# First attention of a two-layer encoder: rope sums bound behind maxima, sum and stacking in separate steps, and the low part of moved pairs on VectorE alone

## The chip, the cores and the metric

The kernel runs on one core of a Trainium2 chip. The metric is the device time of one execution in microseconds, as the median of several runs. The engines are called PE (matmul; PEld is its weight load), DVE (VectorE), ACT (ScalarE), POOL (GpSimd) and SP (SyncE, which here only issues DMAs).

## The reference

An encoder of two layers for one sequence of 1024 tokens with 1024 features in float32. Layer 0 is a differential attention with 8 heads, layer 1 a latent attention (MLA). The change touches layer 0 alone:

```python
proj = h @ w_in                                   # 1024 x 4096
q, k, v, z = split(proj)
q = _rope(q.reshape(b, s, 16, 64), positions)     # 8 heads, two halves of 64 each
k = _rope(k.reshape(b, s, 16, 64), positions)

def block(qb):
    sc = einsum('bqhcd,bkhcd->bhcqk', qb, k) * scale      # c = 0, 1
    p = softmax(sc, axis=-1)
    p = p[:, :, 0] - lam * p[:, :, 1]
    return einsum('bhqk,bkhd->bqhd', p, v)

o = _rmsnorm(o, subln_g) * (1.0 - lambda_init)
o = o.reshape(b, s, 1024) * silu(z)
return o @ w_out

# _rope: concatenate([x1 * cos - x2 * sin, x2 * cos + x1 * sin])
```

## The kernel before

Float32 products run on PE as three matmuls of split operands (`mm3`, L203 to L205): high x high, low x high, high x low. So every operand has a high part, a copy rounded on ACT, and a low part, the difference, on DVE or POOL. For the weights these are `wh` (ACT, L253) and `wl` (POOL, L254). A strip of weights is projected into a PSUM bank `acc`; the strips of the next head's k, q and z are woven as `fill` between the attention tiles of the head before.

A head of layer 0 has eight query tiles of 128 rows, in four pairs `qp`. `q_tile` does for c = 0 and 1 the scores `s` (L905, a PSUM bank of 128x1024 for each c, two in all), the negated maximum `nm` (DVE, L433) and the exponential (ACT, L436; for c = 0 into the tile `e`, for c = 1 in place). The combine (DVE, L911 to L913) then makes p0 - lam x p1 from both, and so is the last reader of the second score bank.

The combined tile must be transposed for the product with v (`pv`). Most pairs go over PE: transposes `tr` (L414), high part `pth` (ACT, L416), low part `ptl` (DVE, L419). The first pair of each half of a head is mostly "moved" (class `Mate`): `move` transposes 32x32 blocks on DVE into `eT` (L1079) and writes them to DRAM, `fetch` reads them back as `pr`, `high` copies the two high halves on ACT (L1097) and, one tile later, `low` subtracts the two low halves, kh = 0 on DVE (L1116) and kh = 1 on POOL (L1113). The pv follows one tile after that. There are 13 moved pairs in layer 0. Layer 1 uses the same class.

A strip of q or k that is done goes through the rope: `rope` copies it to `rp_raw` (ACT, L345 or L347), swaps its quarters by four DMAs into `rp_sw` (L349) and multiplies it by the cosines (POOL, L350). `rot` multiplies the swapped one by the sines (POOL, L355). `fin` adds both on DVE (L359, here "the rope sum"). Then `stack_k` or `stack_q` puts high and low parts into the operand of the scores (`ks`; `qa`, `qb`): copies on ACT (L367, L368, L375, L376), differences on POOL (L369, L370, L377, L378). These steps are spaced by `side`, a queue of which one entry is taken at each tick of the projection stream: three empty ticks, `rot`, three empty ticks, then sum and stacking together.

The engines' orders are set by a list scheduler over the program, with a few bindings. `mk` holds marked instructions, and `behind("V")` lets the next instruction be issued only after the one marked V: at any time the last maximum, low part of a transposed tail, combine, or 32x32 transpose. `in_turn` keeps POOL's instructions in the order of the program.

Of the kernel before, what the change touches and what calls it, by code (L numbers as in the profile page):

```python
# [37 lines left out]
DEF = 7  # L38
ROT = 3
# [54 lines left out]
def f32v(ap):  # L94
    return ap.bitcast(F32)
# [3 lines left out]
def trunk(ctx: ExitStack, tc: tile.TileContext, A, out):  # L99
    nc = tc.nc  # L100
    SP, PE, V, S, G = nc.sync, nc.tensor, nc.vector, nc.scalar, nc.gpsimd
# [29 lines left out]
    def bank(tag, name, shape=None):  # L131
        nonlocal turn
        if tag == "acc":
            turn += 1
            if (turn - 1) % (2 + NB.get("accx", 0)) < 2:
                return psa.tile([P, HF], F32, name=name, tag="acc", bufs=2)
            tag = "accx"
        return ps.tile(shape or [P, HF], F32, name=name, tag=tag, bufs=NB[tag])
# [60 lines left out]
    def pin(ins):  # L199
        return tc.keep_in_program_order(ins) if pinned[0] else ins  # L200
# [9 lines left out]
    mk = {}  # L210

    def behind(eng):

        return tc.issue_after(mk[eng]) if eng in mk else nullcontext()

    def in_turn(ins):

        return tc.keep_in_program_order(ins) if mk else ins
# [105 lines left out]
    side = Side()  # L324
# [13 lines left out]
    def rope(rp, acc, half, scale, eng=G):  # L338

        cs = slice(half * HF, half * HF + HF)  # L340
        raw = rp.tile([P, HF], F32, name="rp_raw", tag="rp", bufs=6)
        sw = rp.tile([P, HF], F32, name="rp_sw", tag="rp", bufs=6)
        r = rp.tile([P, HF], F32, name="rp_r", tag="rp", bufs=6)
        if scale == 1.0:
            S.copy(raw, acc)  # L345
        else:
            S.mul(raw, acc, scale)  # L347
        for q in range(4):
            SP.dma_start(sw[q * 32 : q * 32 + 32], raw[(q ^ 1) * 32 : (q ^ 1) * 32 + 32])  # L349
        r_ = eng.tensor_mul(r, raw, cosT[:, cs])  # L350
        if eng is G:
            in_turn(r_)

        def rot():
            in_turn(G.tensor_mul(sw, sw, sinT[:, cs]))  # L355

        def fin():
            with behind("V"):
                V.tensor_add(r, r, sw)  # L359
            return r  # L360

        return rot, fin

    def stack_k(t, r):

        with behind("S"):
            S.copy(t[0:64, 0, :], r[0:64])  # L367
            S.copy(t[64:128, 1, :], r[64:128])  # L368
        in_turn(G.tensor_sub(t[64:128, 0, :], r[0:64], f32v(t[0:64, 0, :])))  # L369
        in_turn(G.tensor_sub(t[0:64, 1, :], r[64:128], f32v(t[64:128, 1, :])))  # L370

    def stack_q(qa, qb, r, slot=None):

        with behind("S"):
            S.copy(qa[0:64, 0, :], r[0:64])  # L375
            S.copy(qa[64:128, 1, :], r[64:128])  # L376
        in_turn(G.tensor_sub(qb[0:64, 0, :], r[0:64], f32v(qa[0:64, 0, :])))  # L377
        in_turn(G.tensor_sub(qb[64:128, 1, :], r[64:128], f32v(qa[64:128, 1, :])))  # L378

        def swap():  # L380
            for t in (qa, qb):
                for to, at, c in ((slice(64, 128), slice(0, 64), 0), (slice(0, 64), slice(64, 128), 1)):
                    with behind("SP") if slot is not None else nullcontext():
                        SP.dma_start(f32v(t[to, c, :]), f32v(t[at, c, :]))

        if slot is None:
            swap()
        else:
            prep.setdefault(slot, []).append(swap)
# [40 lines left out]
    def softmax_part(ap_, s_ps, zs, bufs, tag="e"):  # L430

        nm = sm.tile([P, 1], F32, name="nm")
        mk["V"] = V.reduce_max(nm, s_ps, axis=AX.X, negate=True).ins  # L433
        e = ap_.tile([P, T], F32, name="e", tag=tag, bufs=bufs) if ap_ else s_ps
        with tc.issue_after(mk.pop("H")) if "H" in mk else nullcontext():
            ex = S.activation(e, s_ps, AF.Exp, bias=nm, scale=1.0, accum_out=zs)  # L436
            pin_last(ex)
            mk["S"] = ex.ins
        return e
# [369 lines left out]

    KS, QS, GZ = {}, {}, {}  # L810

    def k_done(h):
        def f(acc, half):
            rot, fin = rope(wp, acc, half, 1.0, G if h else V)

            def g():
                t = a0a.tile([P, 2, HF], F32R, name="ks", tag="ks", bufs=4)
                stack_k(t, fin())
                KS.setdefault(h, [None, None])[half] = t

            side.add(*[None] * ROT, rot, *[None] * (DEF - 1 - ROT), g)
        return f

    def q_done(h):
        def f(acc, half):
            rot, fin = rope(wp, acc, half, SC0, G if h else V)

            def g():
                qa = a0a.tile([P, 2, HF], F32R, name="qa", tag="qs", bufs=4)
                qb = a0a.tile([P, 2, HF], F32R, name="qb", tag="qs", bufs=4)  # L830
                stack_q(qa, qb, fin(), now[0] + 1 if h and half else None)
                QS.setdefault(h, [None, None])[half] = qa, qb

            side.add(*[None] * ROT, rot, *[None] * (DEF - 1 - ROT), g)
        return f

    def silu_gate(tp, acc):
# [19 lines left out]
    for h in range(NH):  # L857
        items += [(strip0(1, h), h0, k_done(h)), (strip0(0, h), h0, q_done(h)), (strip0(2, h), h0, z_done(h))]
    with tc.issue_after(h_last):
        k_done(0)(kacc, 0)  # L860
# [34 lines left out]
    def q_tile(h, half, ti, zz, ep, mid=lambda i: None, tag="e"):  # L895

        ql = slice(ti * P, (ti + 1) * P)
        zs = [zz[:, ti : ti + 1], sm.tile([P, 1], F32, name="z1")]
        es = []
        qa, qb = QS[h][half]  # L900
        for c in range(2):
            s_ps = bank("sc", "s", [P, T])
            for src, fst in ((qa, True), (qb, False)):
                for kc in range(2):
                    pin(PE.matmul(s_ps[:, kc * HF : (kc + 1) * HF], src[:, c, ql], KS[h][kc][:, c, :], start=fst, stop=not fst))  # L905
            with tc.issue_after(combined[-1]) if c == 0 and combined else nullcontext():
                es.append(softmax_part(None if c else ep, s_ps, zs[c], 1 if ep is a0a or tag != "e" else 2, tag))
            mid(c)
        e0, e1 = es
        z0, z1 = zs  # L910
        V.reciprocal(z1, z1)  # L911
        V.tensor_scalar(z1, z1, z0, neglam[:, 0:1], op0=ALU.mult, op1=ALU.mult)
        combined.append(V.scalar_tensor_tensor(out=e0, in0=e1, scalar=z1[:, 0:1], in1=e0, op0=ALU.mult, op1=ALU.add).ins)  # L913
        if mk:
            mk["V"] = combined[-1]
        return e0

    first, combined = [], []
    for tt in range(8):
        if tt == V_LATE:  # L920
            psum("ps2", sc=2, tr=1, pv=1)
            zz0 = sm.tile([P, 4], F32, name="zz")
            first += [zz0, q_tile(0, 0, 0, zz0, a0a)]
        for _ in range(MODS[tt]):
            next(mods_g)
        for t in pend[2 * tt : 2 + 2 * tt] if tt > 1 else ():
            with tc.issue_after(store_v.last):
                t()
        v0_tile(tt, 1, wv1)
        if tt == HOLD:  # L930
            with tc.issue_after(store_v.last):
                for raw, src in held:
                    SP.dma_start(raw, src)
# [135 lines left out]
    class Mate(Tail):  # L1069
# [6 lines left out]

        def move(self, t, e):
            eT = self.c["pool"].tile([P, D], F32, name="eT", tag="eT", bufs=self.c["nT"])
            mk["V"] = V.transpose(eT.rearrange("p (c k j) -> p c k j", c=4, j=32), e.rearrange("p (k c i) -> p c k i", c=4, i=32)).ins  # L1079
            mk["SP"] = SP.dma_start(self.store[t], eT).ins  # L1080

        def fetch(self):
# [23 lines left out]
        def low(self, eng=V):  # L1106
            if eng is V and self.done:
                return
            self.done = True
            for kh in range(2):  # L1110
                r, (hi, lo) = self.views(kh)
                if kh == 0 if eng is G else kh == 1 and self.c["l"] == 0:
                    in_turn(G.tensor_sub(lo, r, f32v(hi)))  # L1113
                else:
                    with behind("V"):
                        V.tensor_sub(lo, r, f32v(hi))  # L1116

    tails, hooks = [None, None], []
    now, prep, post, due = [0], {}, {}, {}
# [58 lines left out]
    def attn0(h, fills, extra=None, late=None):  # L1178
# [11 lines left out]
        for qp in range(4):  # L1190
# [5 lines left out]
            for t in range(2):  # L1196
# [15 lines left out]
                if early:  # L1212
                    e0 = first.pop()
                else:
                    own = qp % 2 == t == 0
                    e0 = q_tile(h, half, (qp * 2 + t) % 4, zz, a0a if own else a0b, mid, "e" if own or moved or qp % 2 else "eT")
# [968 lines left out]
```

## Time and profile before

| | |
|---|---|
| runs | 1449.73, 1452.91, 1455.47 us (median 1452.91) |
| profiled execution | 1454.32 us, its span 1452.5 us |
| mean granted clock of PE | 0.980 |
| PE busy in the span | 1369.5 us (94%) |
| DVE, ACT, POOL busy | 956.3 (66%), 739.0 (51%), 647.2 (45%) us |
| first attention with its projections | about 144 to 720 us of the span |

A row of the profile names the line, the engine, the operation and the tiles (out<-in, buffer numbers left out). In a timeline row the first two numbers are the start and the duration in us, and a bracket holds the idle time of the engine ahead of the instruction and what ended it. PEclk is the clock granted to PE as a share of full speed.

### The profile page before, as it was taken

The numbers are of one execution on the slowest core, as the hardware profiler recorded it, in microseconds if no ns is written. First come the engines' busy times: TensorE is split into PE (matmuls) and PEld (weight loads), VectorE is DVE, ScalarE is ACT, GpSimd is POOL, SyncE is SP. The second block draws the span as 40 slices with busy tenths as digits, with TensorE's granted clock in tenths as the row PEclk, the third lists the DMA queues.
The fourth block names the chain that finished last, engine by engine and source line by source line (L and its number), as shares of the span: only waits on it lengthen the run. The fifth ranks groups of instructions, "written<-read, shape, count | busy, mean of one in ns | idle before, by whom it ended". The sixth has DMA issues, their size and how long they took to land.

```text
span 1452.5 us, 20216 instructions
## 1 busy us (share of the span) xinstructions
PE 1369.5 (94%) x7046; PEld 1142.3 (79%) x7046; DVE 956.3 (66%) x1352; ACT 739.0 (51%) x1264; POOL 647.2 (45%) x497
## 2 busy tenths in 40 slices
PE   9999889999798899899899999999999999999997
PEld 7778678777687778778778778887888888887886
DVE  7657867776576676777735597515777777664355
ACT  6622356655465555566534555334555555554442
POOL 4325156655474656565364125523133241413562
PEclk9999899999999999899999999999999999999999
DMA  9877845464445355433774313248777887777563
GB/s 350 257 229 239 256 111 143 133 185 119 115 144 157 115 160 145 136 97 102 261 257 142 131 59 108 93 139 240 191 212 205 234 243 202 187 225 232 197 218 143
DMA packets 165624, 258.24 MB, mean 178 GB/s; under 512 B 20369, under 2 KB 85009, under 8 KB 165522
## 3 DMA queue, kind: packets, MB, share of 16 engines
q1 hardware_dynamic: 165522, 256.94, 59.2%
q8 instruction: 56, 0.92, 0.3%
q14 instruction: 46, 0.38, 0.1%
HBM read 159.42 MB, written 73.86 MB: 161 GB/s over the span
## 4 chain that ended last, share of the span: by engine, by line
PE 62%; DVE 11%; DMA 9%; ACT 5%; POOL 5%; issue 5%; SPq 2%; DVEq 0%; POOLq 0%; ACTq 0%
PE s L1872 8%; PE acc L205 6%; PE acc L203 6%; PE acc L204 6%; PE s L905 5%; PE oacc L203 4%; PE oacc L205 4%; PE oacc L204 4%; PE tr L414 3%; PE pv L204 3%; PE pv L205 3%; PE pv L203 3%; DVE nm L433 2%; DVE ada L476 2%; PE zacc L203 1%
## 5 line engine op out<-in xcount | busy, mean ns | idle before, releaser
L433 DVE TENSOR_REDUCE nm<-s 128x1 f32<-128x1024 f32 x192 | 232.8, 1214 | 64.6 <-PE s L905 40.1
L436 ACT ACTIVATE e<-s,nm 128x1024 f32<-128x1024 f32 x128 | 143.1, 1118 | 173.5 <-DVE nm L433 173.1
L254 POOL TENSOR_TENSOR wl<-wraw,wh 128x512 fp32r<-128x512 f32 (+2 forms) x82 | 104.2, 1274 | 127.0 <-ACT wh L253 111.9
L416 ACT CAST pth<-tr 128x512 fp32r<-128x512 f32 x148 | 87.0, 588 | 143.9 <-PE tr L414 143.0
L205 PE MATMUL acc<-h0h,wl 128*128 128x512 f32 x360 | 145.3, 404 | 15.6 <-POOL wl L254 15.6
L204 PE MATMUL pv<-ptl,vt 128*128 128x256 f32 x512 | 147.5, 288 | 8.8 <-POOL ptl L1113 8.7
L203 PE MATMUL acc<-h0h,wh 128*128 128x512 f32 x360 | 149.7, 416 | 2.7 <-DVE v_hl L393 1.7
L203 PE MATMUL pv<-pth,vt 128*128 128x256 f32 x512 | 147.9, 289 | 0.1
L205 PE MATMUL pv<-pth,vt 128*128 128x256 f32 x512 | 146.5, 286 | 0.0
L204 PE MATMUL acc<-h0l,wh 128*128 128x512 f32 x360 | 143.8, 400 | 0.0
L419 DVE TENSOR_TENSOR ptl<-tr,pth 128x512 fp32r<-128x512 f32 x148 | 101.4, 685 | 62.1 <-ACT pth L416 61.4
L1275 POOL TENSOR_TENSOR wol<-wor,woh 128x512 fp32r<-128x512 f32 x64 | 85.6, 1360 | 79.6 <-ACT woh L1274 72.5
L204 PEld LDWEIGHTS pv<-ptl,vt 128*128 128x128 f32 x512 | 99.1, 194 | 14.7 <-POOL ptl L1113 10.0
L414 PE MATMUL tr<-ident,e 128*128 128x128 f32 x592 | 91.1, 277 | 18.8 <-DVE ptl L419 18.5
L414 PEld LDWEIGHTS tr<-ident,e 128*128 128x128 f32 x592 | 71.9, 142 | 44.3 <-DVE ptl L419 18.2
L203 PEld LDWEIGHTS pv<-pth,vt 128*128 128x128 f32 x512 | 98.8, 193 | 5.0 <-ACT pth L416 0.5
L205 PEld LDWEIGHTS pv<-pth,vt 128*128 128x128 f32 x512 | 99.5, 194 | 0.0
L205 PEld LDWEIGHTS acc<-h0h,wl 128*128 128x128 f32 x360 | 69.3, 192 | 34.2 <-POOL wl L254 18.7
L905 PE MATMUL s<-ks,qa 128*128 128x512 f32 x256 | 85.3, 415 | 10.1 <-ACT e L436 4.9
L436 ACT ACTIVATE s<-s,nm 128x1024 f32<-128x1024 f32 x64 | 69.9, 1092 | 30.0 <-DVE nm L433 29.9
L913 DVE SCALAR_TENSOR_TENSOR e<-s,z,e 128x1024 f32<-128x1024 f32 x64 | 82.1, 1284 | 1.8
L905 PE MATMUL s<-ks,qb 128*128 128x512 f32 x256 | 81.8, 401 | 1.6 <-POOL o L965 1.6
(635 smaller groups left out, 3557.1 us busy)
## 6 DMA issues: line engine op xcount, KB each, us to landing
pS<-eT SPq DMA_DIRECT2D x54, 512.0 KB, 3.0
pr<-pS SPq DMA_DIRECT2D x108, 256.0 KB, 5.9
ada<-in_ada_ss SPq DMA_DIRECT2D x32, 512.0 KB, 7.2
wraw<-in_w_s SPq DMA_DIRECT2D x64, 256.0 KB, 3.0
vS<-v_hl SPq DMA_DIRECT2D x32, 512.0 KB, 4.8
vt<-vS SPq DMA_DIRECT2D x32, 512.0 KB, 5.4
wor<-in_w_out SPq DMA_DIRECT2D x64, 256.0 KB, 3.3
rp_sw<-rp_raw SPq DMA_DIRECT2D x168, 64.0 KB, 2.4
```

What stands on the lines that cost most here:

```text
L203: pin(PE.matmul(psum, ah, bh, start=first, stop=False))
L204: pin(PE.matmul(psum, ah, bl, start=False, stop=False))
L205: mm = PE.matmul(psum, al, bh, start=False, stop=last)
L254: sub = (lo_on or (V if pair_of else G)).tensor_sub(l_[:, :n], raw[:, :n], f32v(h_[:, :n]))
L414: pin(PE.transpose(tr[:, j, :], p[:, kt * P : (kt + 1) * P], ident))
L416: cp = S.copy(pth[kh][:, :, dst], tr)
L419: mk["V"] = V.tensor_sub(ptl[kh][:, :, dst], tr, f32v(pth[kh][:, :, dst])).ins
L433: mk["V"] = V.reduce_max(nm, s_ps, axis=AX.X, negate=True).ins
L436: ex = S.activation(e, s_ps, AF.Exp, bias=nm, scale=1.0, accum_out=zs)
L905: pin(PE.matmul(s_ps[:, kc * HF : (kc + 1) * HF], src[:, c, ql], KS[h][kc][:, c, :], start=fst, stop=not fst))
L1275: in_turn(G.tensor_sub(lo, raw, f32v(hi)))
L1872: pin(PE.matmul(s_ps[:, kc * HF : (kc + 1) * HF], lhs, rhs(kc), start=i == 0, stop=i == 4))
```

## The change

Three things change in layer 0.

1. For the heads 1 to 7, `in_two` takes the rope sum out of the entry that stacks: one empty tick after `rot`, the sum; another, the stacking. So the sum is written two ticks earlier in the program, and the stacking where it was. For head 0 nothing changes.
2. The combine and, in layer 0, the 32x32 transpose are marked "C" and no longer "V". The rope sums, bound behind "V", are thus bound behind maxima and tails' low parts only.
3. `Mate.low` in layer 0 does both halves on DVE, bound behind "C". Layer 1 stays as it was.

The core of the diff:

```diff
--- before.py
+++ after.py
@@ -809,29 +809,46 @@
 
     KS, QS, GZ = {}, {}, {}
 
+    def in_two(h, first_, second):
+
+        def both():
+            first_()
+            second()
+
+        if h:
+            side.add(None, first_, None, second)
+        else:
+            side.add(*[None] * (DEF - 1 - ROT), both)
+
     def k_done(h):
         def f(acc, half):
             rot, fin = rope(wp, acc, half, 1.0, G if h else V)
 
+            r = []
+
             def g():
                 t = a0a.tile([P, 2, HF], F32R, name="ks", tag="ks", bufs=4)
-                stack_k(t, fin())
+                stack_k(t, r[0])
                 KS.setdefault(h, [None, None])[half] = t
 
-            side.add(*[None] * ROT, rot, *[None] * (DEF - 1 - ROT), g)
+            side.add(*[None] * ROT, rot)
+            in_two(h, lambda: r.append(fin()), g)
         return f
 
     def q_done(h):
         def f(acc, half):
             rot, fin = rope(wp, acc, half, SC0, G if h else V)
 
+            r = []
+
             def g():
                 qa = a0a.tile([P, 2, HF], F32R, name="qa", tag="qs", bufs=4)
                 qb = a0a.tile([P, 2, HF], F32R, name="qb", tag="qs", bufs=4)
-                stack_q(qa, qb, fin(), now[0] + 1 if h and half else None)
+                stack_q(qa, qb, r[0], now[0] + 1 if h and half else None)
                 QS.setdefault(h, [None, None])[half] = qa, qb
 
-            side.add(*[None] * ROT, rot, *[None] * (DEF - 1 - ROT), g)
+            side.add(*[None] * ROT, rot)
+            in_two(h, lambda: r.append(fin()), g)
         return f
 
     def silu_gate(tp, acc):
@@ -912,7 +929,7 @@
         V.tensor_scalar(z1, z1, z0, neglam[:, 0:1], op0=ALU.mult, op1=ALU.mult)
         combined.append(V.scalar_tensor_tensor(out=e0, in0=e1, scalar=z1[:, 0:1], in1=e0, op0=ALU.mult, op1=ALU.add).ins)
         if mk:
-            mk["V"] = combined[-1]
+            mk["C"] = combined[-1]
         return e0
 
     first, combined = [], []
@@ -1076,7 +1093,7 @@
 
         def move(self, t, e):
             eT = self.c["pool"].tile([P, D], F32, name="eT", tag="eT", bufs=self.c["nT"])
-            mk["V"] = V.transpose(eT.rearrange("p (c k j) -> p c k j", c=4, j=32), e.rearrange("p (k c i) -> p c k i", c=4, i=32)).ins
+            mk["V" if self.c["l"] else "C"] = V.transpose(eT.rearrange("p (c k j) -> p c k j", c=4, j=32), e.rearrange("p (k c i) -> p c k i", c=4, i=32)).ins
             mk["SP"] = SP.dma_start(self.store[t], eT).ins
 
         def fetch(self):
@@ -1109,10 +1126,10 @@
             self.done = True
             for kh in range(2):
                 r, (hi, lo) = self.views(kh)
-                if kh == 0 if eng is G else kh == 1 and self.c["l"] == 0:
+                if eng is G and kh == 0:
                     in_turn(G.tensor_sub(lo, r, f32v(hi)))
                 else:
-                    with behind("V"):
+                    with behind("V" if self.c["l"] else "C"):
                         V.tensor_sub(lo, r, f32v(hi))
 
     tails, hooks = [None, None], []
```

Line numbers behind the first place of the diff are larger by 17 now (the combine L913 is L930, the low part L1116 is L1133, the transpose L1079 is L1096). POOL's list loses 13 rows, the `ptl<-pr,pth` of the moved pairs; what is left keeps its order but for a few neighbours. PE's order stays as it was but for two swaps of neighbours.

DVE at the seventh tile of head 0, before: the low half of a moved pair, the transpose of the next moved tile, the two maxima of a tile with a rope sum between them, then the combine.

```order
L1116 TENSOR_TENSOR ptl<-pr,pth 128x1024
L1079 STREAM_TRANSPOSE eT<-e 128x1024
L433 TENSOR_REDUCE nm<-s 128x1
L359 TENSOR_TENSOR rp_r<-rp_r,rp_sw 128x512
L433 TENSOR_REDUCE nm<-s 128x1
L911 RECIPROCAL z_1847<-z_1847 128x1
L912 TENSOR_SCALAR z_1847<-z_1847,zz,neglam 128x1
L913 SCALAR_TENSOR_TENSOR e<-s,z_1847,e 128x1024
```

DVE at the same place now:

```order
L1133 TENSOR_TENSOR ptl<-pr,pth 128x1024 x2
L1096 STREAM_TRANSPOSE eT<-e 128x1024
L359 TENSOR_TENSOR rp_r<-rp_r,rp_sw 128x512
L433 TENSOR_REDUCE nm<-s 128x1 x2
L928 RECIPROCAL z_1848<-z_1848 128x1
L929 TENSOR_SCALAR z_1848<-z_1848,zz,neglam 128x1
L930 SCALAR_TENSOR_TENSOR e<-s,z_1848,e 128x1024
L433 TENSOR_REDUCE nm<-s 128x1
```

The second low half has come in, and the rope sum stands ahead of both maxima.

DVE in head 2, from the second maximum of the tile that follows a moved pair, before (L911 to L913 are the combine):

```order
L911 RECIPROCAL z_3237<-z_3237 128x1
L912 TENSOR_SCALAR z_3237<-z_3237,zz,neglam 128x1
L913 SCALAR_TENSOR_TENSOR e<-s,z_3237,e 128x1024
L359 TENSOR_TENSOR rp_r<-rp_r,rp_sw 128x512
L433 TENSOR_REDUCE nm<-s 128x1
L1025 TENSOR_TENSOR sl_f<-zz 128x4
```

DVE at the same place now:

```order
L433 TENSOR_REDUCE nm<-s 128x1 x2
L359 TENSOR_TENSOR rp_r<-rp_r,rp_sw 128x512
L928 RECIPROCAL z_3237<-z_3237 128x1
L929 TENSOR_SCALAR z_3237<-z_3237,zz,neglam 128x1
L930 SCALAR_TENSOR_TENSOR e<-s,z_3237,e 128x1024
L433 TENSOR_REDUCE nm<-s 128x1 x2
```

The rope sum, which stood behind the combine, stands ahead of it, directly behind the maxima.

ACT in head 5, from the exponentials of a tile to the high part of a weight strip, before (`zth` is the tanh of the gate, `qa` the stacking of q):

```order
L436 ACTIVATE e,zz<-s,nm 128x1024
L436 ACTIVATE s,z_4895<-s,nm 128x1024
L375 CAST qa<-rp_r 64x512
L376 CAST qa<-rp_r 64x512
L841 ACTIVATE zth<-acc 128x512
L253 CAST wh<-wraw 128x512
```

ACT at the same place now:

```order
L436 ACTIVATE e,zz<-s,nm 128x1024
L416 CAST pth<-tr 128x4x128
L436 ACTIVATE s,z_4895<-s,nm 128x1024
L858 ACTIVATE zth<-acc 128x512
L375 CAST qa<-rp_r 64x512
L376 CAST qa<-rp_r 64x512
L253 CAST wh<-wraw 128x512
```

The tanh has gone ahead of the two `qa` copies, and a tail's copy between the exponentials.

## The prediction

> **What bounds the kernel now.** First the page (busy time by engine), then the waits of PE, the stretches and the groups of instructions, all for the first attention (144 to 720 us), where the whole change lies; at last the order of time around each wait of PE there.
>
> ```profile
> PE 1369.5 (94%) x7046; PEld 1142.3 (79%) x7046; DVE 956.3 (66%) x1352; ACT 739.0 (51%) x1264; POOL 647.2 (45%) x497
> ```
>
> PE is busy for 94%. So no engine's total can decide here, only the gaps and the slow clock of PE. The waits, "engine line <- released by: us in total, times, longest":
>
> ```profile
> PE acc L205 <- POOL wl L254: 15.6, 6, 6.9
> PE tr L414 <- DVE ptl L419: 10.8, 8, 3.0
> PE pv L204 <- POOL ptl L1113: 8.7, 3, 3.3
> PE s L905 <- ACT e L436: 4.9, 4, 1.8
> PE ssq L1022 <- ACT rp_raw L347: 4.1, 2, 3.0
> ```
>
> The instruction that the change takes off POOL (L1113) releases PE three times, 8.7 us. POOL's weight splits cost more, 15.6 us. The stretches (busy us and instructions of each engine, granted clock, DMA):
>
> ```profile
> 206.04:209.45 3.41, 3.41 (x13) 3.02 (x13) 2.82 (x2) 1.01 (x2) 2.13 (x3) 0.50 0.34 109
> 345.99:352.81 6.82, 6.21 (x20) 5.44 (x21) 2.51 (x2) 2.17 (x4) 6.82 (x6) 0.50 0.29 77
> 209.50:345.90 136.40, 127.02 (x683) 107.20 (x681) 105.66 (x139) 82.43 (x140) 78.52 (x62) 1.00 0.55 148
> 144.00:720.00 576.00, 520.49 (x2717) 435.79 (x2715) 412.51 (x549) 321.72 (x545) 317.28 (x245) 0.96 0.53 149
> ```
>
> PE idles 576.00 - 520.49 = 55.5 us here. Between those two stalls the clock is 1.00; behind them it is 0.50 for 3.41 and 6.82 us. At half the clock, half of PE's busy time is lost: 3.41/2 + 6.21/2 = 4.8 us. DVE is busy 412.5 of 576, so 13 more subtractions fit in its total; where they stand decides. The groups (out<-in xcount | busy, mean ns | idle before, releaser):
>
> ```profile
> L1113 POOL TENSOR_TENSOR ptl<-pr,pth 128x1024 fp32r<-128x1024 f32 x13 | 31.7, 2442 | 12.9 <-ACT pth L1097 12.8
> L359 DVE TENSOR_TENSOR rp_r<-rp_r,rp_sw 128x512 f32<-128x512 f32 x28 | 26.7, 954 | 24.6 <-POOL rp_sw L355 24.6
> L1116 DVE TENSOR_TENSOR ptl<-pr,pth 128x1024 fp32r<-128x1024 f32 x13 | 22.5, 1734 | 0.0
> ```
>
> **The change, part by part.** POOL loses 13 x 2.442 = 31.7 us; DVE gains 13 x 1.2 to 1.73 = 16 to 22 us (bounds: the quickest row of L1116, below, and its mean). And DVE's rope sums, which wait 24.6 us for POOL's products in all, move in its order, two ticks earlier and past combines or maxima: whoever stood behind no sum now stands behind a waiting one. No instruction or DMA is added; PE's order hardly changes. I went through the places where PE waits, with the new order on the old durations.
>
> A, head 0, tile 6:
>
> ```profile
> 200.40 1.18 DVE L433 TENSOR_REDUCE nm<-s 128x1 f32<-128x1024 f32 x1
> 206.63 1.75 DVE L359 TENSOR_TENSOR rp_r<-rp_r,rp_sw 128x512 f32<-128x512 f32 x1 [5.04 <-POOL rp_sw L355]
> 203.02 2.33 POOL L1113 TENSOR_TENSOR ptl<-pr,pth 128x1024 fp32r<-128x1024 f32 x1
> 205.31 1.28 POOL L355 TENSOR_TENSOR rp_sw<-rp_sw,sinT 128x512 f32<-128x512 f32 x1
> 205.41 0.39 PE L204 MATMUL pv<-ptl,vt 128*128 128x256 f32 x1 [3.34 <-POOL ptl L1113]
> 208.71 0.97 PE L905 MATMUL s<-ks,qa 128*128 128x512 f32 x2
> ```
>
> The stall of 3.34 goes. But the sum now stands ahead of the maximum of 200.40. Without L1113 the product ends at 203.02 + 1.28 = 204.3, the sum 0.7 to 1.75 later (205 to 206), the maximum at 206.2 to 207.2, the exponential that frees the score bank 1.1 after that. So the scores of 208.71 start at about 208.3, whatever PE saved ahead of them. They gain 0.4; the new stall, of about 4 us, costs clock behind it, as the old one did (up to 1.7, I take 0.8): **+0.4** (bounds -1.5 to +2).
>
> B, head 1:
>
> ```profile
> 275.21 0.39 PE L204 MATMUL pv<-ptl,vt 128*128 128x256 f32 x1 [2.32 <-POOL ptl L1113]
> 277.68 2.01 DVE L359 TENSOR_TENSOR rp_r<-rp_r,rp_sw 128x512 f32<-128x512 f32 x1 [2.27 <-POOL rp_sw L355]
> ```
>
> The stall of 2.32 goes; the sum comes ahead of the combine, which stood ahead of it. With L1113's 2.33 off POOL's queue the sum ends at 276 to 277.4, the combine at 278 to 279.2, and frees the second score bank then. Of 2.32 remain **-1.0** (bounds -2.3 and 0).
>
> C, head 2:
>
> ```profile
> 344.40 1.28 DVE L913 SCALAR_TENSOR_TENSOR e<-s,z,e 128x1024 f32<-128x1024 f32 x1
> 350.29 2.04 DVE L359 TENSOR_TENSOR rp_r<-rp_r,rp_sw 128x512 f32<-128x512 f32 x1 [4.61 <-POOL rp_sw L355]
> 344.20 2.34 POOL L1113 TENSOR_TENSOR ptl<-pr,pth 128x1024 fp32r<-128x1024 f32 x1
> 346.60 0.58 PE L204 MATMUL pv<-ptl,vt 128*128 128x256 f32 x1 [3.04 <-POOL ptl L1113]
> 354.52 0.63 PE L905 MATMUL s<-ks,qa 128*128 128x512 f32 x2
> ```
>
> Stall and slow clock go: 3.04 + 6.21/2 = 6.1 us, so PE would be at the scores of 354.52 by 348.4. Their bank is freed by the combine, now behind the sum: 350.3 - 2.3 = 348.0 for its start, done at 348.7 to 350.0, combine at 350.5 to 351.8. PE waits 2.1 to 3.4: **-3.2** (bounds -6.1 and -2.7).
>
> D, POOL's weight splits, heads 3 to 5:
>
> ```profile
> 376.27 1.22 DVE L1116 TENSOR_TENSOR ptl<-pr,pth 128x1024 fp32r<-128x1024 f32 x1
> 376.45 2.17 POOL L378 TENSOR_TENSOR qb<-rp_r,qa 64x512 fp32r<-64x512 f32 x1
> 380.02 0.79 PE L205 MATMUL acc<-h0h,wl 128*128 128x512 f32 x1 [6.90 <-POOL wl L254]
> 454.81 0.50 PE L205 MATMUL acc<-h0h,wl 128*128 128x512 f32 x1 [4.79 <-POOL wl L254]
> 533.05 0.50 PE L205 MATMUL acc<-h0h,wl 128*128 128x512 f32 x1 [1.77 <-POOL wl L254]
> 450.53 0.60 ACT L841 ACTIVATE zth<-acc 128x512 f32<-128x512 f32 x1
> ```
>
> In these three the split comes ahead of L1113 in POOL's queue already, so nothing is gained. But the qb subtraction beside L1116 takes 2.17 where the same form takes 1.28 (the L355 row, twice the partitions): DVE's subtraction of two SBUF operands and POOL's hold each other up. A second one just behind the first does it again, about 1.05 each time, 3.2 in all (bounds 0 and 3 x 1.22). In heads 4 and 5 ACT's order also sets the gate's tanh (0.60) ahead of the exponential or of the qa casts; that, and what it waits for itself, I put at 0.9 each (0.6 to 1.5). **+5.0** (bounds 0 and +6.7).
>
> The Trainium skill bears on this ("SBUF — State Buffer", section "SBUF: two separate sides"): the port pair that VectorE and GpSimd share is an exclusive lock, held for a whole instruction, when a VectorE instruction with two SBUF inputs meets a GpSimd one that reads SBUF. The trace agrees in kind (2.17 for 1.28). By the rule each second subtraction would cost its full 1.22, and the sum would be 0.5 us higher.
>
> E, heads 4 and 5, where L1113 delayed no one:
>
> ```profile
> 502.42 1.28 DVE L913 SCALAR_TENSOR_TENSOR e<-s,z,e 128x1024 f32<-128x1024 f32 x1
> 505.62 1.76 DVE L359 TENSOR_TENSOR rp_r<-rp_r,rp_sw 128x512 f32<-128x512 f32 x1 [1.92 <-POOL rp_sw L355]
> 505.63 0.62 PE L905 MATMUL s<-ks,qa 128*128 128x512 f32 x2
> 575.10 1.23 DVE L433 TENSOR_REDUCE nm<-s 128x1 f32<-128x1024 f32 x1 [0.69 <-PE s L905]
> 581.27 1.74 DVE L359 TENSOR_TENSOR rp_r<-rp_r,rp_sw 128x512 f32<-128x512 f32 x1 [4.94 <-POOL rp_sw L355]
> 578.05 1.11 ACT L436 ACTIVATE e<-s,nm 128x1024 f32<-128x1024 f32 x1
> ```
>
> In head 4 the combine of 502.42 falls behind the sum of 505.62: done at 508.1 or later, so the scores of 505.63 start 2.5 later; a wait of 1.06 behind them takes some of it: **+1.5** (bounds 0 and 2.5). In head 5 the maximum of 575.10 falls behind the sum of 581.27, and its exponential of 578.05 with it. Both ran while DVE and ACT were free; now 1.23 + 1.11 = **+2.3** lies on the way to the next scores (bounds 0 and 3.8).
>
> F, earlier maxima and tails, no longer behind a combine or a transpose:
>
> ```profile
> 184.62 0.63 PE L414 MATMUL tr<-ident,e 128*128 128x128 f32 x4 [1.31 <-DVE ptl L419]
> 234.85 0.73 PE L905 MATMUL s<-ks,qa 128*128 128x512 f32 x2 [1.33 <-ACT e L436]
> ```
>
> Of 184.62 I credit 0.9 and of 234.85 all 1.3. Of the wait group tr <- ptl (10.8 over 8), what is left without 1.31 and the longest is 6.5 over six, 1.1 each; the new order serves two of these, 1.7. **-3.9** (bounds -5 and 0).
>
> Sum: 0.4 - 1.0 - 3.2 + 5.0 + 1.5 + 2.3 - 3.9 = **+1.1 us**. The profiled execution took 1454.32 us (its span 1452.5), the median of the runs is 1452.91, 1.4 below; so 1455.4 there, and 1454.0 on the median's scale.
>
> **The rivals.** R1, nobody misses DVE: the waits on L1113 (8.7), the clock behind two of them (4.8) and F (3.9) all come back, and the port costs nothing: 1452.9 - 17.4 = 1435.5. For it: DVE has 160 us free here, and a sum that no longer waits for L1113 is ready 2.3 us sooner. Against it: in A, B and C the sum still waits, by up to 3 us, with a maximum or combine behind it. It decides if POOL's products are done before the combine or maximum is. By the Trainium skill ("TensorE: Matmul & The Clock Gate", Part 1) the clock halves after an idle window of about 3.4 us; rows here show 0.50 behind stalls of 3.34 and 3.04, so the measurement decides; by the rule the 4.8 would not come back, and R1 would be 1440.3.
>
> R2, the sums hold up the maxima: the five waits above (5.04, 2.27, 4.61, 1.92, 4.94) sum to 18.8; less 3 x 2.33 for L1113 gone, 11.8 lands on PE in full, D adds 5.0, the stalls of 8.7 go, and new stalls of over 3 us in A, C and E cost 1.7 of clock each: 1452.9 + 11.8 + 5.0 - 8.7 + 5.1 = 1466.1. For it: PE's reserve of scores is two banks, and both need DVE. Against it: the sum is placed two ticks before its stacking, and at most other tiles its product is long done. It decides from about 3 us of wait per place.
>
> R3, a hidden change: one of several engines off the bound swaps work with another, all waits go round; 1453. It lies with my own forecast.
>
> **How the numbers follow.** The forecast and R3 0.45 (own range 1446 to 1460), R1 or most of it 0.27, R2 or most of it 0.28. About 0.5%, 7.3 us, is what a measurement here tells from no change: below 1445.6 is faster, above 1460.2 slower; the three cases fall in the three bands. The range cuts the outer third of R1 and R2: 1439 to 1469.
>
> **What would show it.** Right: no PE wait on ptl from the moved pairs; L1116's form x26, with mean 1.2 to 1.7; PE's waits s <- ACT e up from 4.9 to about 10, s <- DVE e to 6, acc <- wl from 15.6 to 18 or more; clock still 0.50 behind 206, not behind 346. Wrong: DVE's idle time before L359 falling from 24.6 under 10 (then R1), or rising over 35 with maxima late by it (then R2).

## The result, and the profile after

The changed kernel takes 1465.48 us in the median (1464.35 to 1466.12, three runs), the kernel before 1452.91. The ratio is 1.009, with a 95% interval of 1.0072 to 1.0108: slower by 0.9%, about 13 us. The forecast was 1454.0; the rival R2 (sums that hold up maxima, 1466.1) is what came. In a run further down, one execution of `split_marks` (1518.65 us, at a granted clock of 0.852) is left out of the ratio.

The page of the profile after, busy time by engine (its span is 1464.3 us):

```profile
PE 1371.3 (94%) x7046; PEld 1141.8 (78%) x7046; DVE 973.0 (66%) x1365; ACT 736.8 (50%) x1264; POOL 622.8 (43%) x484
```

The work was moved as the code says: DVE 956.3 to 973.0 us with 13 instructions more, POOL 647.2 to 622.8 with 13 fewer. PE's busy time is almost the same, so most of the loss is idle time. The waits of PE in the first attention, now about 144 to 734 us:

```profile
PE acc L205 <- POOL wl L254: 21.0, 6, 7.8
PE s L922 <- DVE e L930: 12.8, 8, 3.6
PE tr L414 <- DVE ptl L419: 10.8, 9, 3.0
PE s L922 <- ACT e L436: 9.1, 3, 3.8
PE ssq L1039 <- ACT rp_raw L347: 7.0, 1, 7.0
```

One row of before, for the waits on combines, was not shown yet:

```profile
PE s L905 <- DVE e L913: 3.1, 2, 2.2
```

The 8.7 us that PE waited for POOL's low half are gone. In their place the scores wait 12.8 + 9.1 = 21.9 us for combines and exponentials (3.1 + 4.9 = 8.0 before), the weight splits cost 5.4 us more and ACT's `rp_raw` 2.9 more. That is 22.2 more and 8.7 less, and with smaller waits that ended the idle time is 590.00 - 523.26 = 66.7 us for 55.5, as the stretch shows:

```profile
355.17:358.58 3.41, 3.41 (x12) 2.74 (x11) 2.07 (x4) 2.13 (x5) 3.33 (x3) 0.50 0.74 212
144.00:734.00 590.00, 523.26 (x2715) 435.22 (x2713) 430.97 (x562) 320.41 (x546) 293.69 (x232) 0.95 0.52 146
```

The first of these rows is behind the new wait in head 2: the clock is at 0.50 again, nine us later than before, and for 3.41 us where it was 6.82. The second is 14.0 us longer than the stretch of 576.00 before: 11.2 us of idle time, and 2.8 us by which PE is busy longer, at a mean clock of 0.95 for 0.96.

The same places in PE's order of time, after, and then five rows of before that stand for the second, third and last three:

```profile
207.73 0.73 PE L922 MATMUL s<-ks,qa 128*128 128x512 f32 x2 [3.83 <-ACT e L436]
281.76 0.70 PE L922 MATMUL s<-ks,qa 128*128 128x512 f32 x2 [2.15 <-DVE e L930]
306.09 0.73 PE L922 MATMUL s<-ks,qa 128*128 128x512 f32 x2 [2.80 <-ACT e L436]
354.37 0.70 PE L922 MATMUL s<-ks,qa 128*128 128x512 f32 x2 [3.65 <-DVE e L930]
382.42 0.79 PE L205 MATMUL acc<-h0h,wl 128*128 128x512 f32 x1 [7.76 <-POOL wl L254]
459.48 0.79 PE L205 MATMUL acc<-h0h,wl 128*128 128x512 f32 x1 [7.08 <-POOL wl L254]
541.95 0.50 PE L205 MATMUL acc<-h0h,wl 128*128 128x512 f32 x1 [4.30 <-POOL wl L254]
598.40 1.87 PE L1039 MATMUL ssq<-ones,osq 128*128 128x1 f32 x8 [6.99 <-ACT rp_raw L347]
656.85 0.66 PE L414 MATMUL tr<-ident,e 128*128 128x128 f32 x4 [2.27 <-DVE ptl L419]
726.41 0.50 PE L204 MATMUL oacc<-wol,oth 128*128 128x512 f32 x1 [1.69 <-POOL wol L1292]
```

```profile
280.30 0.62 PE L905 MATMUL s<-ks,qa 128*128 128x512 f32 x2
304.27 0.73 PE L905 MATMUL s<-ks,qa 128*128 128x512 f32 x2 [1.32 <-ACT e L436]
584.98 1.87 PE L1022 MATMUL ssq<-ones,osq 128*128 128x1 f32 x8 [3.05 <-ACT rp_raw L347]
645.71 0.63 PE L414 MATMUL tr<-ident,e 128*128 128x128 f32 x4 [1.76 <-DVE ptl L419]
712.94 0.50 PE L204 MATMUL oacc<-wol,oth 128*128 128x512 f32 x1 [1.70 <-POOL wol L1275]
```

The start of one and the same matmul in both traces gives how far the changed kernel is behind at that point. Beside it stands what the forecast's terms add up to there.

| the same matmul | before | after | behind by | forecast |
|---|---|---|---|---|
| scores behind A | 208.71 | 207.73 | -1.0 | -1.3 |
| scores behind B | 280.30 | 281.76 | +1.5 | -2.8 |
| scores, head 2 | 304.27 | 306.09 | +1.8 | -3.7 |
| scores behind C | 354.52 | 354.37 | -0.2 | -7.7 |
| D, head 3 | 380.02 | 382.42 | +2.4 | -6.7 |
| D, head 4 | 454.81 | 459.48 | +4.7 | -4.7 |
| D, head 5 | 533.05 | 541.95 | +8.9 | -1.3 |
| E, head 5 | 584.98 | 598.40 | +13.4 | +1.1 |
| head 6 | 645.71 | 656.85 | +11.1 | +1.1 |
| end of the first attention | 712.94 | 726.41 | +13.5 | +1.1 |

In the order of DVE the sum and who stands behind it, at A, C and E (head 5):

```profile
204.62 0.69 DVE L359 TENSOR_TENSOR rp_r<-rp_r,rp_sw 128x512 f32<-128x512 f32 x1 [2.52 <-POOL rp_sw L355]
205.22 2.35 DVE L433 TENSOR_REDUCE nm<-s 128x1 f32<-128x1024 f32 x2
...
350.53 1.99 DVE L359 TENSOR_TENSOR rp_r<-rp_r,rp_sw 128x512 f32<-128x512 f32 x1 [3.90 <-POOL rp_sw L355]
...
352.94 1.28 DVE L930 SCALAR_TENSOR_TENSOR e<-s,z,e 128x1024 f32<-128x1024 f32 x1
...
590.75 1.75 DVE L359 TENSOR_TENSOR rp_r<-rp_r,rp_sw 128x512 f32<-128x512 f32 x1 [3.91 <-POOL rp_sw L355]
592.42 2.34 DVE L433 TENSOR_REDUCE nm<-s 128x1 f32<-128x1024 f32 x2
```

At A two maxima, at C a combine (it began at 344.40 before, now at 352.94), in head 5 two maxima stand behind a sum that waits 2.5 to 3.9 us for POOL's product. And by groups:

```profile
L1133 DVE TENSOR_TENSOR ptl<-pr,pth 128x1024 fp32r<-128x1024 f32 x26 | 44.5, 1750 | 0.0
L1096 DVE STREAM_TRANSPOSE eT<-e 128x1024 f32<-128x1024 f32 x26 | 32.1, 1235 | 0.2
L359 DVE TENSOR_TENSOR rp_r<-rp_r,rp_sw 128x512 f32<-128x512 f32 x28 | 25.0, 893 | 27.4 <-POOL rp_sw L355 27.3
```

DVE's wait ahead of the sums is 27.4 us, for 24.6 before. This small difference hides two larger ones, as the runs below show: with the low half alone moved to DVE the wait falls to 10.4 us, and the marks and the early step raise it again. So longer waits can be what costs, and so can who stands behind them.

### The profile page after: what moved, and what is told of

Same layout as the page of the kernel before. It is cut to its first block, busy times and chain, and to the rows that moved or that the text cites. A ratio compares the mean times of both kernels' runs of the same rounds, so it can differ in the third digit from the quotient of the medians.

```text
span 1464.3 us, 20190 instructions
## 1 busy us (share of the span) xinstructions
PE 1371.3 (94%) x7046; PEld 1141.8 (78%) x7046; DVE 973.0 (66%) x1365; ACT 736.8 (50%) x1264; POOL 622.8 (43%) x484
## 4 chain that ended last, share of the span: by engine, by line
PE 61%; DVE 12%; DMA 9%; POOL 6%; issue 5%; ACT 5%; SPq 2%; POOLq 0%; DVEq 0%; ACTq 0%
PE s L1889 8%; PE acc L205 6%; PE acc L203 6%; PE acc L204 6%; PE s L922 4%; PE oacc L203 4%; PE oacc L204 3%; PE oacc L205 3%; PE tr L414 3%; PE pv L204 3%; PE pv L203 3%; PE pv L205 3%; DVE nm L433 2%; POOL wl L254 2%; DVE e L930 1%
## 5 line engine op out<-in xcount | busy, mean ns | idle before, releaser
L922 PE MATMUL s<-ks,qa 128*128 128x512 f32 x256 | 85.7, 417 | 22.5 <-DVE e L930 12.8
L205 PEld LDWEIGHTS acc<-h0h,wl 128*128 128x128 f32 x360 | 69.9, 194 | 40.3 <-POOL wl L254 24.6
L203 PEld LDWEIGHTS acc<-h0h,wh 128*128 128x128 f32 x360 | 70.5, 196 | 17.2 <-DVE v_hl L393 2.1
L930 DVE SCALAR_TENSOR_TENSOR e<-s,z,e 128x1024 f32<-128x1024 f32 x64 | 82.1, 1283 | 1.8
```

The lines of the kernel that those rows point to most:

```text
L203: pin(PE.matmul(psum, ah, bh, start=first, stop=False))
L205: mm = PE.matmul(psum, al, bh, start=False, stop=last)
```

## Experiments

The theories. S: a rope sum that waits for POOL now stands ahead of maxima and combines, and the scores pay. P: the second subtraction on DVE costs, because it and POOL's subtractions hold each other up just where PE waits for POOL's weight splits. Each run is compared with the kernel before on the same chip (its medians were 1451.4 to 1452.6). A trace is of one execution, and executions of one kernel differ (`split`: 1445.12 to 1455.88 us, of which the last is traced, at a granted clock of 0.974). Where a trace is far from its kernel's median, its own time is given.

### The parts alone

`low_only` undoes the early sum and the marks, and keeps the low half on DVE (cut short here):

```diff
-        if h:
-            side.add(None, first_, None, second)
-        else:
-            side.add(*[None] * (DEF - 1 - ROT), both)
+        side.add(*[None] * (DEF - 1 - ROT), both)
-            mk["C"] = combined[-1]
+            mk["V"] = combined[-1]
-            mk["V" if self.c["l"] else "C"] = V.transpose(...)
+            mk["V"] = V.transpose(...)
-                    with behind("V" if self.c["l"] else "C"):
+                    with behind("V"):
```

> The kernel before with one part of the change: the low half kh=1 of moved pairs on VectorE (bound behind the old mark); rope sums and marks as before. Theory S (the sums cost: a rope sum that waits for POOL now stands ahead of maxima and combines): with the sums where they were, the three waits on L1113 (8.7 us) and part of the slow clock come back and nothing else does: 1440 to 1447. Theory P (the second subtraction on VectorE costs, by the port that it shares with POOL ahead of the weight splits, and by VectorE's time): the six wl waits go from 15.6 to about 21 us as in the changed kernel, and most of the gain is eaten: 1451 to 1458.

1453.91 us, ratio 1.0011 (1.0001 to 1.0020). The three waits on L1113 are gone, and nothing is won. Its waits, and the group of the sums:

```profile
PE acc L205 <- POOL wl L254: 19.7, 6, 7.8
PE s L920 <- ACT e L436: 7.1, 4, 2.8
PE s L920 <- DVE e L928: 5.2, 6, 2.5
```

```profile
L359 DVE TENSOR_TENSOR rp_r<-rp_r,rp_sw 128x512 f32<-128x512 f32 x28 | 25.2, 901 | 10.4 <-POOL rp_sw L355 10.4
```

The weight splits took 4.1 us of the 8.7, the scores 4.3 (7.1 + 5.2 for 8.0). That is theory P for the first half, and for the second simply that PE, come earlier, waits for the next maxima. This trace is of the longest of eleven executions (1457.97 us): up to the end of the first attention, at 719.47 us, PE idles 54.5 us for 55.5 in the trace of the kernel before, and is busy 7.6 us longer (521.0 for 513.4), at a mean clock of 0.975 for 0.980 over the span. So it shows where PE waits; its total is not that of the median. The 14.2 us less that DVE waits ahead of the sums bring no time here; why is open.

`sums_only` is the rest: the changed kernel with the low half kh=1 back on POOL.

```diff
-                if eng is G and kh == 0:
+                if kh == 0 if eng is G else kh == 1 and self.c["l"] == 0:
```

> The kernel before with the rope sum as a step of its own two ticks earlier and with the mark C for combines and transposes; the low half kh=1 stays on POOL. Theory S: the sums wait even longer, since L1113 is still ahead of their products on POOL: slower than the changed kernel or like it, 1463 to 1472, with waits s <- e (combine) of 10 us or more. Theory P: about as before, 1450 to 1457, wl waits at 15.6.

1461.53 us, 1.0065 (1.0049 to 1.0080). Most of the loss comes with the sums and their marks, 9.4 us of 13. It is somewhat less than theory S said, and the waits on combines rose only to 6.1 us. In its trace (1462.76 us) the scores wait 10.8 us for combines and exponentials, for 8.0 before. Up to the end of the first attention PE idles 4.4 us longer than before and is busy 5.1 us longer, at a mean clock of 0.975. So waiting scores are a part of the loss only, and about as much is a slower PE.

`early_only` is `sums_only` with the old marks, `marks_only` is `sums_only` with sum and stacking in one step (the edits above, singly).

> The kernel before with the sum two ticks earlier alone; marks as before, so a sum can't pass the last combine or transpose, low half on POOL. Theory S: the harm needs both the early step and the freed mark; where a combine came just ahead the sum stays behind it, so 1452 to 1462. Theory P: 1450 to 1457.

> The kernel before with the marks alone: combines and transposes marked C, the sum and the stacking in one step as before, low half on POOL. Theory S: the sum is written in its old place, so it passes few combines: 1450 to 1460. Theory P: 1450 to 1457.

`early_only`: 1456.88 us, 1.0037 (1.0021 to 1.0053). `marks_only`: 1453.49 us, 1.0010 (0.9999 to 1.0022), not told from no change. The early step alone costs 0.4%, the mark alone 0.1%, both 0.65%. That the mark lets an early sum pass what held it back is read from the order; these times do not show it, for by their intervals 0.65% can be the mere sum of both. Both runs lie in the ranges of both theories, so they do not decide between them. With the low half on POOL the early step adds 2.0 us to DVE's wait ahead of the sums (27.8 in `marks_only`, 29.8 in `sums_only`) and 8 us to the time; there it is mostly who stands behind. `early_only` (traced at 1460.79 us) also shows a place that the forecast had not looked at, in head 6, where the sum comes ahead of a maximum and a tail's low part (rows of `early_only`, then one of before):

```profile
644.02 2.81 DVE L359 TENSOR_TENSOR rp_r<-rp_r,rp_sw 128x512 f32<-128x512 f32 x1
642.98 3.31 POOL L1130 TENSOR_TENSOR ptl<-pr,pth 128x1024 fp32r<-128x1024 f32 x1
647.50 0.90 PE L414 MATMUL tr<-ident,e 128*128 128x128 f32 x3 [3.28 <-DVE ptl L419]
```

```profile
645.48 1.10 DVE L359 TENSOR_TENSOR rp_r<-rp_r,rp_sw 128x512 f32<-128x512 f32 x1
```

It ran into POOL's low half there, took 2.81 us for its usual 0.7, and PE waited 3.28 us for the `ptl` behind it (1.76 before). The changed kernel lost 1.8 us in head 6 too, at the next tail. There a sum that waited stands ahead of the tail's low part, and PE waits for that; before, it did not wait at this matmul (658.26):

```profile
667.68 1.77 DVE L359 TENSOR_TENSOR rp_r<-rp_r,rp_sw 128x512 f32<-128x512 f32 x1 [0.97 <-POOL rp_sw L355]
671.25 0.66 PE L414 MATMUL tr<-ident,e 128*128 128x128 f32 x4 [1.68 <-DVE ptl L419]
```

### How far the sum stands from the stacking

`low_marks` is the changed kernel with sum and stacking in one step again (four ticks after the product); `later` has the sum at three ticks, where the change has it at two.

```diff
-            side.add(None, first_, None, second)
+            side.add(None, None, first_, second)      # later
```

> The changed kernel with the rope sum back in the step of the stacking, two ticks later; marks and low half as changed. Theory S (the place of the sum is what costs): about the sum of the single parts, 1452.3 + 1.6 (low half) + 1.2 (marks) = 1455, so 10 us under the changed kernel, with the waits s <- e (combine) back from 12.8 to 7 us or less. Theory P (the second subtraction on VectorE and the port cost, the sums only move the wait): 1460 or more.

> The changed kernel with the sum one tick later, one tick ahead of the stacking. Theory S: between the changed kernel and the one with both in one step, 1456 to 1462, the less the more combines stand ahead of the sum again. Theory P: as the changed kernel, 1463 to 1467.

`low_marks`: 1453.67 us, 1.0012 (1.0000 to 1.0023). `later`: 1457.10 us, 1.0028 (1.0017 to 1.0039). So 1.0012, 1.0028, 1.0090 with the sum at four, three and two ticks, as theory S has it. One thing was expected wrongly: in `low_marks` the waits on combines hardly fall; what falls against the changed kernel are the waits on exponentials, 9.1 to 4.9 us, and DVE's wait ahead of the sums:

```profile
PE s L920 <- DVE e L928: 12.3, 9, 3.4
PE s L920 <- ACT e L436: 4.9, 3, 3.0
```

```profile
L359 DVE TENSOR_TENSOR rp_r<-rp_r,rp_sw 128x512 f32<-128x512 f32 x28 | 23.2, 827 | 18.1 <-POOL rp_sw L355 18.1
```

That wait is 18.1, 20.0 and 27.4 us with the sum at four, three and two ticks: with the low half on DVE it grows by 9.3 us while the time grows by 11. Up to the end of the first attention the changed kernel's trace is 11.4 us behind that of `low_marks` (726.41 for 715.05). Of this 8.7 are idle time of PE, most of it ahead of scores that wait for exponentials (4.2), of `rp_raw` (2.8) and of tails' low parts (1.5); 2.7 are busy time. The waits on combines alone need not cost: `low_marks` has 12.3 us of them and `low_only` 5.2, and both take 0.1% more than the kernel before.

### The wait itself

In `free_after` the sum adds the swapped tile as the DMA left it. POOL's product with the sines keeps its size and its place, but writes to a tile that no one reads. So the rotation is left out of the result, not out of POOL's time. `free_before` is the same edit in the kernel before.

```diff
-            in_turn(G.tensor_mul(sw, sw, sinT[:, cs]))
+            in_turn(G.tensor_mul(raw if early else sw, sw, sinT[:, cs]))   # early: heads 1 to 7
```

> The changed kernel in which the rope sum adds the swapped tile as the DMA left it, and POOL's product with the sines goes into the dead rp_raw, of the same size and at the same place of its queue (so the rotation is left out of the result, not out of POOL's time). The sum no longer waits for POOL's product. Theory S as a wait (what costs is that maxima and combines stand behind a sum that waits for POOL): most of the 11 us that the early sum adds come back, 1452 to 1457, and the idle time ahead of the sum falls from 27.4 to under 10 us. Theory S as mere time (the sum's own 0.7 to 2 us ahead of them costs): 1461 to 1466.

> The control: the same edit in the kernel before. There the sums stand behind the combines, and their wait of 24.6 us holds up mostly the stacking. Theory S as a wait: little to gain, 1447 to 1453, so that the gap between both kernels shrinks from 13 to some 5 us. If the wait itself cost as much in the old order: 1440 to 1445, and the gap stays.

`free_after`: 1444.64 us, 0.9952 (0.9939 to 0.9966). `free_before`: 1442.12 us, 0.9939 (0.9919 to 0.9958). The group of the sum in the one and in the other:

```profile
L359 DVE TENSOR_TENSOR rp_r<-rp_r,rp_sw 128x512 f32<-128x512 f32 x28 | 26.9, 961 | 2.9 <-DMA rp_sw<-rp_raw 2.0 <-POOL rp_r L350 0.9
```

```profile
L359 DVE TENSOR_TENSOR rp_r<-rp_r,rp_sw 128x512 f32<-128x512 f32 x28 | 30.1, 1074 | 2.5 <-POOL rp_r L350 1.4 <-DMA rp_sw<-rp_raw 1.1
```

With the wait away, the changed kernel wins about 20 us (1.0090 to 0.9952) and the one before about 9, and the gap between them goes from 0.9% to 0.13%. The sum still stands ahead of maxima and combines (directly ahead of one for 17 of the 28 sums, in the changed kernel for 18) and takes as long (893 to 961 ns). So its place alone costs little, for by their intervals the 0.13% are not told from nothing; its wait for POOL at this place is the price. Both gains are larger than expected, and `free_before` has the time of one of its two cases and the gap of the other: even in the old order that wait cost 9 us. There, too, a maximum stands directly behind five of the seven sums that wait for over 1 us. Up to the end of the first attention the traces have 15.9 us less of idle time of PE and 6.8 less of busy time in the changed kernel (66.5 to 50.6, 515.9 to 509.1), 4.0 and 4.5 less in the one before (55.5 to 51.5, 513.4 to 508.9). The busy time falls with the slow clock: its mean over the span is 0.984 for 0.977 and 0.983 for 0.980. DVE's order also differs in some rows between `free_after` and the changed kernel, since a sum that is ready sooner is set sooner; this part isn't told apart from the wait.

### The port and the weight splits

`split_after` is the changed kernel, `split` the kernel `low_only`, each with the low half kh=1 back on POOL for the second moved pair of a head. That pair's subtraction falls beside the qb and wl subtractions of D.

```diff
+                if kh == 0 if eng is G else kh == 1 and self.c["l"] == 0 and self.qp:
```

> The changed kernel with the low half kh=1 back on POOL for the second moved pair of a head (its subtraction falls on the next head's second tile, beside the qb and wl subtractions); on VectorE only for the first pair. Theory P: the wl waits go back from 21.0 to about 16 us and 4 to 6 us come back: 1459 to 1462. If the port plays no part there, and only the sums count: 1463 to 1467.

> The kernel before with the low half kh=1 on VectorE only for the first moved pair of a head, where POOL's one held PE up three times (8.7 us); sums and marks as before. Theory P: the wl waits stay at 15.6, the three waits on POOL's low half are gone, and with part of them given back at the next scores 4 to 7 us remain: 1445 to 1449. If the waits that replace them take all of it: 1451 to 1454.

`split_after`: 1459.67 us, 1.0051 (1.0037 to 1.0066). `split`: 1448.05 us, 0.9977 (0.9963 to 0.9991), faster than both kernels. Both times are as theory P has it, 5 to 6 us each. The waits for the weight splits fell less than it said, to 18.4 us for about 16 and to 17.1 for 15.6. That is 2.6 us in each, about half of the gain; the other half is not traced to its places. The rows at D in head 3, changed kernel, and then the one of before for the weight splits:

```profile
377.82 3.42 DVE L1133 TENSOR_TENSOR ptl<-pr,pth 128x1024 fp32r<-128x1024 f32 x2
377.99 2.16 POOL L378 TENSOR_TENSOR qb<-rp_r,qa 64x512 fp32r<-64x512 f32 x1
380.23 3.37 POOL L254 TENSOR_TENSOR wl<-wraw,wh 128x512 fp32r<-128x512 f32 x2
```

```profile
378.70 2.50 POOL L254 TENSOR_TENSOR wl<-wraw,wh 128x512 fp32r<-128x512 f32 x2
```

The two engines take turns: qb behind the first low half, the second low half (2.2 us for 1.22) behind qb, the first wl behind that. Two wl take 3.37 us for 2.50: 0.87 on the way of PE (3.36 and 3.38 at the same place in heads 4 and 5). The transposes of DVE, which read one tile, took 1.235 us in the mean beside the same POOL. `split` keeps seven of the 13 moved subtractions, and its weight splits wait 17.1 us for 19.7 in `low_only`. At the three places of D PE waits 6.89, 6.22 and 2.12 us in `split` for 7.75, 7.08 and 2.98 in `low_only`: 0.86 less at each, the same figure a second time. The group in `split`, and then head 4 in `low_only` and in `split`:

```profile
L1131 DVE TENSOR_TENSOR ptl<-pr,pth 128x1024 fp32r<-128x1024 f32 x20 | 32.3, 1641 | 0.0
```

```profile
457.84 0.80 PE L205 MATMUL acc<-h0h,wl 128*128 128x512 f32 x1 [7.08 <-POOL wl L254]
```

```profile
455.28 0.80 PE L205 MATMUL acc<-h0h,wl 128*128 128x512 f32 x1 [6.22 <-POOL wl L254]
```

### Two tries to go on from `split`

`split_marks` adds the marks C; `split_late` sets sum and stacking together one tick later than before.

```diff
+            side.add(*[None] * (DEF - ROT), both)      # split_late, from head 1 on
```

> The kernel before with the marks C and with the low half kh=1 on VectorE for the first moved pair of a head alone, sum and stacking in one step. If the marks help once the low half is moved (1.6 + 1.2 became 1.0 us together): 1445 to 1448. If they are neutral or cost their 1.2: 1448 to 1450.

> The kernel before with the low half kh=1 on VectorE for the first moved pair of a head alone, and from head 1 on with sum and stacking together one tick later than before (the opposite direction of the change). Theory S as a wait: later sums wait less for POOL's products, and some of the 9 us that the wait costs in the kernel before come back, unless the scores then wait for the stacked operand: 1440 to 1447. If the stacking has no tick to spare: 1450 to 1460, with PE waits s <- qa by DMA.

`split_marks`: 1452.55 us, 1.0006 (0.9993 to 1.0020), worse than either expectation: the free mark costs about 0.3% here. `split_late`: 1456.09 us, 1.0024 (1.0012 to 1.0036). So the stacking seems to have no tick to spare. The scores wait 7.9 us for the stacked q (2.1 in the kernel before, 2.8 in `split`), and 7.9 for combines (4.5 in `split`). But this trace is of the shortest of eleven executions (1447.79 us), 8.3 us under the median; it shows these waits, and not the whole loss:

```profile
PE s L922 <- DMA qa<-qa: 7.9, 5, 3.0
```

## Why the prediction was wrong in its likeliest case

The time lies in the stated range, near its upper end; the likeliest case, no change that can be told, did not come, and R2 did, with a chance of 0.28 and 1466.1 us. Of the signs named for the likeliest case the moved pairs' missing wait, the exponentials (9.1 us for about 10) and the weight splits (21.0 for 18 or more) came; the waits on combines (12.8 for 6) and the clock in head 2 did not.

- A, at its scores, came as worked out: -1.0 for -1.3, with the new wait of 3.83 us for "about 4". The slow clock behind it cost 1.2 for 0.8.
- F is the term that failed by its logic. The four waits it credits did end: between them the changed kernel catches up by 1.2 to 1.5 us at each. But it loses that again at the next transposes and scores, in part by waits of 0.1 to 0.4 us: behind B it is 1.5 us late for -2.8, and in head 2 a wait of 2.80 us took the place of 1.32, with a clock of 0.50 behind it that cost 1.5 more. `low_only` has a wait of 2.8 there too, so it is not the sums': PE, come earlier, stood where the next maximum was not ready. A wait ahead of another wait was credited as if the second were not there.
- B and C went the way that was said, with new waits of 2.15 and 3.65 us, and the sizes were off: the sum took 2.0 us in both (the upper bound), and half of the slow clock that C was to win back came again behind the new wait (0.50 from 355.17, for 3.41 us where it was 6.82). From A's scores to C's the forecast had -6.4, the trace +0.8; that is 7.2 of the 12.4 us by which it was short.
- D was right in its mechanism and somewhat small: the three splits wait 0.9, 2.3 and 2.5 us more (7.76, 7.08, 4.30 for 6.90, 4.79, 1.77), 5.7 for 5.0. The port's part is 0.87 each, near the 1.05 taken; of the two prices that the forecast weighed, 1.22 and 1.05, it is nearer the lower. Of the rest, 1.4 in head 4 comes with the low half of the first pairs (6.22 in `split` for 4.79), and 1.3 in head 5 with the sums and marks (4.30 for 2.98 in `low_only`); the forecast put this down to ACT's order, which no run tests alone. The rows agree in kind with the exclusive lock that the Trainium skill states ("SBUF — State Buffer", "SBUF: two separate sides").
- E in head 4 was a wait of 1.06 us at the scores (514.85) for 2.5; from D in head 4 to D in head 5 4.2 us were lost for 3.4. E in head 5: the wait for `rp_raw` grew from 3.05 to 6.99 us, and 1.6 of it came back at the next scores (588.91 before, 600.70 after); from D in head 5 to there 2.9 were lost for the forecast 2.3. Head 6 was not looked at and was put at nothing: there the changed kernel lost 2.4 us more (10.6 us late where the head begins to fall back, 13.0 after it), and `early_only` falls back by 6.1 us in its profiled execution, by the same comparison of matmul starts.
- What would show R2 was named wrongly: "idle time before L359 over 35". It was 27.4, though far over the 10.4 of `low_only`. The sign was in the waits of the scores, 21.9 us for 8.0.
- R2's time fits, its terms but partly: the scores wait 13.9 us more for 11.8, the splits 5.4 more for 5.0, PE's busy time grew by 2.8 (523.26 - 520.49) where 5.1 of slow clock were put. So it is partly by luck that 1466.1 lies so near the 1465.5 measured.
- R1 fell by both its conditions: the sums were not ready before the combines, and the port was not free. `free_after` shows a part of what it would have taken: without the wait for POOL the time is 1444.6, still 9 us over R1.

## What to carry to other kernels

Before an instruction that waits for another engine is moved ahead in an in-order queue, look at what will stand behind it: the wait need not grow much to cost more (2.0 us of wait and 8 us of time, with the low half on POOL). Look also at whether what it waits for is done by then: with the low half on DVE the early step added 9.3 us of wait and 11 us of time. A wait that goes away is worth only what lies between it and the next one that still ends at the same time, so follow the gain to the next place where PE asks for something. And work that is moved between two engines that hold each other up can be moved by place: here it paid for the first pair of a head and cost for the second.

## What was not expected of the hardware

A clock of 0.50 came behind waits shorter than those of the prediction. The stretches around the wait of 2.80 us at 306.09 and around that of 2.15 us at 281.76, in the changed kernel:

```profile
303.97:307.38 3.41, 1.29 (x6) 1.07 (x7) 1.28 (x2) 2.06 (x4) 0.61 (x1) 1.00 0.62 155
307.38:310.79 3.41, 3.41 (x10) 2.63 (x9) 3.41 (x4) 0.00 (x0) 0.95 (x1) 0.50 0.00 0
282.00:307.00 25.00, 22.20 (x120) 18.59 (x120) 17.16 (x27) 15.80 (x27) 13.19 (x13) 1.00 0.64 169
280.08:283.49 3.41, 1.73 (x8) 1.42 (x9) 3.17 (x4) 3.34 (x7) 3.33 (x3) 1.00 0.73 208
```

Behind 2.80 us the clock is low, though PE was busy for 1.29 of the 3.41 us ahead; behind the 2.15 us at 281.76, with 1.73 of 3.41 us busy, it stays at 1.00. The Trainium skill ("TensorE: Matmul & The Clock Gate", Part 1) has an idle window of about 3.4 us ahead of half clock; here the measurement decides: a stretch that is idle in part was enough. And VectorE's subtractions and GpSimd's alternated one by one when both had several in a row, each taking up to 2.2 us for 1.2 to 1.3.
